# A two-layer hybrid encoder on one core: the norms' 1 / rms through ScalarE's logarithm and exponential instead of Newton steps on VectorE

## The chip, the cores and the metric

The kernel runs on one core of a Trainium2 chip. A core has TensorE (PE, matrix products, with its weight loads listed apart as PEld), VectorE (DVE), ScalarE (ACT), GpSimd (POOL) and SyncE (SP, which here only issues DMAs), each with its own in-order queue of instructions. SBUF holds the working tiles (128 partitions), PSUM the results of TensorE, in banks of 128 x 512 float32. The metric is the device time of one execution in microseconds (us).

## The reference

Two layers of an encoder over 1024 tokens of width 1024, all in float32, and a last norm. Cut to what matters:

```python
def rms_norm(x, g):
    y = x * lax.rsqrt(jnp.mean(x * x, axis=-1, keepdims=True) + EPS)     # EPS = 1e-6
    return y * g

for l in range(DEPTH):                                   # DEPTH = 2
    proj = rms_norm(x, norm1_g[l]) @ w_in[l]
    (a_cq, a_ckv, a_kr, b_q, ..., d_v) = jnp.split(proj, splits, axis=-1)
    y_a = mla_mixer(...)    # latent attention: rms_norm(a_cq) over 192 and rms_norm(a_ckv) over 128 columns first
    y_b = diff_mixer(...)   # w = p0 - lam * p1 per head; rms_norm of each head's 64 outputs, no norm of the group
    y_c = swa_mixer(...)    # window of +-128
    y_d = na_mixer(...)     # 2-D neighbourhood
    mix = concatenate([rms_norm(y_a), y_b, rms_norm(y_c), rms_norm(y_d)])
    x = x + mix @ w_out[l]
    x = x + square(relu(rms_norm(x, norm2_g[l]) @ w_up[l])) @ w_down[l]
return rms_norm(x, final_norm_g)
```

So each layer has norm1, two latent norms, the two pairs of B's heads, the norms of groups A, C and D, and norm2; the final norm closes the kernel.

## The kernel before

Activations lie with features on partitions and the 1024 tokens along the free dimension, eight tiles of 128 x 1024. Every product of float32 operands is made of three passes over a high and a low part of each operand (`passes`, L220 to L222); `split` (L194, L197, L198, and L188, the line of every two-operand operation) makes the parts, the high one on ScalarE, the low one on VectorE or, for weights, on GpSimd.

A layer runs in stages. Projection of group B's six column tiles in two waves (`several`). Attention of B (`attn_b`), and woven into it, as filling, the projections of the latents (`proj_latent`) and of group D. Then attention of D with the projections of C and the latents' up-projections (`latent_up`), attention of C, attention of A, the output projection, and the MLP (`mlp_up`, `mlp_down`), in which sums of blocks replace an eighth of the block products. `weave` takes turns between an attention and its filling; `tick` lets the steps of finished heads (`tails`: `denominators`, `sub_norm`, `mix_group`, `mix_b`) follow one at a time. The written order is not the last word: the kernel is put in order by a planner that simulates the engines with estimated durations before the kernel runs, and so fixes the order of each engine's queue. Only TensorE's order in the MLP is left as written.

A norm over features needs sums across partitions. The squares are summed over the tiles first; `rstd_cols` then multiplies each 128 tokens of them by a column of ones (L261), so that PSUM holds one column per 128 tokens, tokens on partitions: 8 columns for the whole sequence, 16 for two heads at once, 4 for half the sequence. The mean and the small constant are applied on VectorE (L263, or L688 for the latents). `rsqrt_cols` then takes 1 / sqrt of the columns: a first value from the bits of the number (L247, an integer shift in float arithmetic) and three Newton steps of three VectorE operations each (L249, L188, L251). The columns come back to rows in one of two ways. `spread_here` multiplies a broadcast column by the identity (L297) and copies the bank to SBUF (L292): norm1, norm2 and, in `final`, the last norm. `rows_of` transposes the columns (L270), copies (L272) and stores them in DRAM, and `spread` loads the rows broadcast over partitions: the latents, `sub_norm` and `mix_group`.

The latents' sums come from `latent_parts` (L655 and L657) as three small tiles of 8 columns: two of the query latent, to be added, and one of the key-value latent. `proj_latent` ends with both norms (L688 to L689) and stores two sets of rows.

In B's attention, `probs` makes two softmaxes per query tile. `softmax` writes negated scores and their minimum `nm` in one pass on VectorE (L806), after which ScalarE takes the exponential with its sum (L809). The second head's probabilities are scaled by `cb` = z0 * (-lam) / z1, one number per row: a reciprocal (L890) and one more operation (L891) on VectorE, the scaling on ScalarE (L893), the sum on GpSimd. That is 64 times in the kernel.

The functions used on ScalarE are copy, square and exponential; the one table load stands at the kernel's start.

Of the kernel before, what the change touches and what calls it, by code (L numbers as in the profile page):

```python
# [6 lines left out]

# [1 line left out]

# [4 lines left out]
F = mybir.dt.float32  # L14
R = mybir.dt.float32r
I32 = mybir.dt.int32
AF = mybir.ActivationFunctionType
# [6 lines left out]
EPS = 1e-6  # L24
NEG = -1e30
LAYERS = 2


T_CQ, T_CQR, T_CKV = 0, 1, 2
# [116 lines left out]
class Trunk:  # L146
# [91 lines left out]
                                    c == 0 and k == 0, c == 1 and k == 3)  # L238


    def rsqrt_cols(self, ms):

        nc = self.nc
        n = ms.shape[1]
        r = self.cp.tile([P, n], F, tag="rs_r", name="rs_r")
        t = self.cp.tile([P, n], F, tag="rs_t", name="rs_t")
        nc.vector.tensor_scalar(r.bitcast(I32), ms.bitcast(I32), -0.5, 1597463007.0, ALU.mult, ALU.add)  # L247
        for _ in range(3):
            nc.vector.scalar_tensor_tensor(out=t, in0=r, scalar=-0.5, in1=r, op0=ALU.mult, op1=ALU.mult)  # L249
            self.tt(t, t, ms)  # L250
            nc.vector.scalar_tensor_tensor(out=r, in0=t, scalar=1.5, in1=r, op0=ALU.add, op1=ALU.mult)  # L251
        return r

    def rstd_cols(self, sq, count, rhs, tag="mm"):

        nc = self.nc
        g = rhs.shape[1]
        n = sq.shape[1] // P
        ps = self.bank(tag, [P, n * g])
        for t in range(n):  # L260
            nc.tensor.matmul(ps[:, t * g:(t + 1) * g], sq[:, t * P:(t + 1) * P], rhs, start=True, stop=True)  # L261
        ms = self.cp.tile([P, n * g], F, tag="ms", name="ms")
        nc.vector.tensor_scalar(ms, ps, 1.0 / count, EPS, ALU.mult, ALU.add)  # L263
        return self.rsqrt_cols(ms)

    def rows_of(self, col, grid=False):

# [12 lines left out]

    def spread(self, dst, rows, j=0, g=1):

        src = rows.rearrange("(t g) p -> g t p", g=g)[j]
        n = dst.shape[0]
        self.load(dst.rearrange("p (t q) -> p t q", t=8), src.partition_broadcast(n))

    def spread_here(self, dst, col):

# [12 lines left out]
    def setup(self):  # L301
        nc, d = self.nc, self.d
        tile = lambda shape, name, dt=F: self.const.tile(shape, dt, name=name)
        width = d["par"].shape[1]
        par = tile([P, width], "par")
        self.load(par, d["par"])
        self.x, self.first = [], []
        for k in range(8):
            if k < 3:
                self.first.append(self.weights(d["w_in"][0, self.WAVES[0][k], 0]))  # L310
            x = self.xp.tile([P, S], F, tag="x", name=f"x{k}")
            self.load(x, d["x"][k])
            self.x.append(x)
        self.ident = tile([P, P], "ident")
        self.load(self.ident, d["ident"])
        self.ones = tile([P, 2], "ones")
        nc.vector.memset(self.ones, 1.0)
        self.pairs = tile([P, 2], "pairs")
        nc.vector.memset(self.pairs, 0.0)
        nc.vector.memset(self.pairs[0:64, 0:1], 1.0)  # L320
        nc.vector.memset(self.pairs[64:128, 1:2], 1.0)
        self.rb = tile([P, S], "rb")
        self.zero = tile([P, P], "zero", R)
        nc.vector.memset(self.zero.bitcast(F), 0.0)

        at = 0

        def take(*shape):
            nonlocal at
            n = math.prod(shape)  # L330
            v = par[:, at:at + n]
            at += n
            return v.rearrange("p (l k) -> p l k", l=shape[0]) if len(shape) > 1 else v

        L = LAYERS
        self.g1, self.g2, self.gfin = take(L, 8), take(L, 8), take(8)
        self.gout = {n: take(L, 2) for n in ("mla", "swa", "na")}
        self.gkv, self.gq, gsub, self.sink = take(L), take(L, 2), take(L), take(L, 4)
        self.nsink = tile([P, L, 4], "nsink")
        nc.vector.tensor_scalar(self.nsink, self.sink, -1.0, None, ALU.mult)  # L340
        lam = self.rb.rearrange("p (l f) -> p l f", l=L)[:, :, 0:256]
        self.load(lam[:, :, 0:128], d["lam"].rearrange("p (l f) -> p l f", l=L))
        self.gsub = tile([P, L], "g_sub")
        self.nlam = tile([P, L], "nlam")
        e = tile([P, L, 2], "lam_e")
        for l in range(L):
            li = 0.8 - 0.6 * math.exp(-0.3 * l)
            nc.vector.tensor_scalar(self.gsub[:, l:l + 1], gsub[:, l:l + 1], 1.0 - li, None, ALU.mult)
            v = lam[:, l, 128:192]
            self.tt(v, lam[:, l, 0:64], lam[:, l, 64:128])  # L350
            nc.vector.tensor_reduce(out=e[:, l], in_=v.rearrange("p (j f) -> p j f", j=2), axis=AX, op=ALU.add)
            nc.scalar.activation(e[:, l], e[:, l], AF.Exp)
            nc.vector.tensor_scalar(e[:, l, 0:1], e[:, l, 0:1], li, None, ALU.add)
            self.tt(self.nlam[:, l:l + 1], e[:, l, 1:2], e[:, l, 0:1], ALU.subtract)
# [306 lines left out]
    def proj_latent(self, l, one, xs, rb, tabs, lat, krd, rows_out):  # L661


        nc = self.nc
        squares = [self.col("sq%d" % i, 8) for i in range(3)]
        for i, t, g in ((0, T_CQ, self.gq[:, l, 0:1]), (2, T_CKV, self.gkv[:, l:l + 1])):
            yield from one(t, xs, self.ev_plain(rb, lambda n, y: self.latent_parts(y, g, P, n, lat[:, i], squares[i])))
        c, s = tabs

        def ev(n, ps):  # L670
            sl = slice(n * 512, n * 512 + 512)
            y, t2 = self.part(), self.part()
            self.tt(y[0:64], ps[0:64], rb[0:64, sl])
            self.tt(y[64:112], ps[64:112], c[64:112, sl])
            self.tt(t2[64:80], ps[96:112], s[96:112, sl])
            self.tt(t2[96:112], ps[64:80], s[64:80, sl])
            self.tt(y[64:80], y[64:80], t2[64:80], ALU.add, self.eng)
            self.tt(y[96:112], y[96:112], t2[96:112], ALU.subtract, self.eng)
            self.emit_parts(y[64:112], [
                (krd[:, :, h, sl].rearrange("a p s -> p a s"), slice(64 + 32 * h, 80 + 32 * h))  # L680
                for h in range(2)], slice(64, 112))
            self.latent_parts(y, self.gq[:, l, 1:2], 64, n, lat[:, 1], squares[1])

        yield from one(T_CQR, xs, ev)
        q, k = squares[0], squares[2]
        self.tt(q, q, squares[1], ALU.add)
        for m, count in ((q, 192), (k, 128)):
            nc.vector.tensor_scalar(m, m, 1.0 / count, EPS, ALU.mult, ALU.add)  # L688
            rows_out.append(self.rows_of(self.rsqrt_cols(m)))  # L689
        yield True  # L690

    def latent_up(self, l, lat, rows, qa, ka, va):
        nc, d = self.nc, self.d
        rq, rkv = self.big_tile(F, "rq"), self.big_tile(F, "rkv")
        self.spread(rq, rows[0])
        self.spread(rkv, rows[1])
        parts = []
        for i, r in ((0, P), (1, 64), (2, P)):
            p = []
# [165 lines left out]
    def attn_b(self, l, t, qb, kb, vb, out):  # L865
# [3 lines left out]
        def head(h2):  # L869
            if h2 == 0:  # L870
                pair["y"], pair["rz"] = self.ypair(), self.rz_tile()
            y, rz = pair["y"], pair["rz"]
            qk = []
            for c in range(2):
                g = h2 * 2 + c
                q, k = self.stack(), self.stack()
                qf, kf = q.bitcast(F), k.bitcast(F)
                for i, (a, b) in enumerate(((0, 0), (0, 1), (1, 0))):
                    self.load(qf[i * 32:(i + 1) * 32], run(qb[a, t, g]))
                    self.load(kf[i * 32:(i + 1) * 32], run(kb[b, t, g]))  # L880
                qk.append([(q[0:96], k[0:96])])
            v = self.vtile(vb[2 * t + h2])
            z = [self.col("z0", 8), self.col("z1", 8)]

            def probs(qt):
                ps = []
                for c in range(2):
                    ps.append(self.softmax(qk[c], qt, z[c][:, qt:qt + 1], 32 ** -0.5))
                c = self.col("cb")
                nc.vector.reciprocal(c, z[1][:, qt:qt + 1])  # L890
                nc.vector.scalar_tensor_tensor(out=c, in0=z[0][:, qt:qt + 1], scalar=self.nlam[:, l:l + 1], in1=c,  # L891
                                               op0=ALU.mult, op1=ALU.mult)
                nc.scalar.activation(ps[1], ps[1], AF.Copy, scale=c)  # L893
                self.tt(ps[0], ps[0], ps[1], ALU.add, nc.gpsimd)
                return ps[0]

            def done():
                self.tails.append(self.denominators(z[0], rz[h2 * 64:(h2 + 1) * 64]))

            return probs, v, y, h2, done  # L900
# [590 lines left out]
```

## Time and profile before

| | |
|---|---|
| median of 3 runs | 2735.67 us (2726.91 to 2736.3) |
| the profiled execution | 2728.97 us |
| its span, first to last instruction | 2727.2 us |
| mean granted TensorE clock | 0.967 |
| busy: TensorE, VectorE, ScalarE, GpSimd | 2553.1, 1994.1, 1430.9, 1134.5 us |

The rows that follow in the prediction are of four kinds. The first part of the page gives the busy time of each engine with its share of the span and the number of instructions; the fourth gives the shares of the chain of work that ended last. A row of the windows view gives a stretch (start:end, length) and then, for TensorE, its weight loads, VectorE, ScalarE and GpSimd, the busy time with the number of instructions, followed by the granted clock, the share of the DMA engines and GB/s; its last row is the sum. A row of the timeline gives start, duration, engine, line, operation, output<-inputs, shapes and, in brackets, how long the engine stood idle before it and what ended that. A row of the grouped instructions gives count | busy us, mean ns of one | idle time before. The view of one source line gives its durations in ns as least/median/greatest, and who waited for it (us, times).

### The profile page before, as it was taken

The numbers are of one execution on the slowest core, as the hardware profiler recorded it, in microseconds if no ns is written. First come the engines' busy times: TensorE is split into PE (matmuls) and PEld (weight loads), VectorE is DVE, ScalarE is ACT, GpSimd is POOL, SyncE is SP. The second block draws the span as 40 slices with busy tenths as digits, with TensorE's granted clock in tenths as the row PEclk, the third lists the DMA queues.
The fourth block names the chain that finished last, engine by engine and source line by source line (L and its number), as shares of the span: only waits on it lengthen the run. The fifth ranks groups of instructions, "written<-read, shape, count | busy, mean of one in ns | idle before, by whom it ended". The sixth has DMA issues, their size and how long they took to land.

```text
span 2727.2 us, 37613 instructions
## 1 busy us (share of the span) xinstructions
PE 2553.1 (94%) x12298; PEld 2110.1 (77%) x12298; DVE 1994.1 (73%) x3544; ACT 1430.9 (52%) x2547; POOL 1134.5 (42%) x754
## 2 busy tenths in 40 slices
PE   8989988899989999999999899889998999999997
PEld 6778876787778887888877688767886788878886
DVE  7787767674966669787567778677749666687786
ACT  4667757563534444444436676576635344444444
POOL 2555642111245554445435556331013455545552
PEclk9989999999989999999998899899999999999998
DMA  5534597231234447444244345972221444664431
GB/s 175 166 105 126 154 280 241 83 93 40 65 130 156 151 160 267 156 138 142 98 133 138 95 134 157 300 215 71 76 70 44 154 159 149 223 222 150 131 100 62
DMA packets 190516, 389.20 MB, mean 143 GB/s; under 512 B 23712, under 2 KB 30832, under 8 KB 190320
## 3 DMA queue, kind: packets, MB, share of 16 engines
q1 hardware_dynamic: 176496, 361.62, 43.0%
q10 hardware_dynamic: 13824, 25.17, 2.7%
q8 instruction: 98, 1.61, 0.3%
q14 instruction: 98, 0.80, 0.1%
HBM read 263.29 MB, written 123.41 MB: 142 GB/s over the span
## 4 chain that ended last, share of the span: by engine, by line
PE 70%; DVE 14%; DMA 7%; ACT 4%; issue 3%; SPq 1%; POOL 1%; DVEq 0%; ACTq 0%; POOLq 0%
PE u L220 8%; PE u L222 8%; PE u L221 8%; PE mm L220 5%; PE mm L221 5%; PE mm L222 5%; PE p L220 5%; PE p L221 5%; PE p L222 5%; PE sb L804 3%; PE tr L840 2%; DVE p L806 2%; DVE part L188 2%; PE pv L829 2%; PE pv L828 2%
## 5 line engine op out<-in xcount | busy, mean ns | idle before, releaser
L188 POOL TENSOR_TENSOR wl<-raw,wh 128x512 fp32r<-128x512 f32 x448 | 635.1, 1418 | 705.2 <-ACT wh L194 690.1
L194 ACT ACTIVATE wh<-raw 128x512 fp32r<-128x512 f32 x448 | 281.5, 629 | 579.8 <-PE u L221 315.0
L188 POOL TENSOR_TENSOR wl<-ws,wh 128x512 fp32r<-128x512 f32 (+1 forms) x112 | 148.1, 1325 | 456.9 <-ACT wh L194 426.0
L220 PE MATMUL u<-far,wh 128*128 128x512 f32 x768 | 301.5, 393 | 11.5 <-ACT ev L1237 8.3
L188 DVE TENSOR_TENSOR raw<-raw 128x512 f32<-128x512 f32 x256 | 226.4, 890 | 107.4 <-POOL wl L188 56.9
L222 PE MATMUL u<-far,wl 128*128 128x512 f32 x768 | 300.5, 391 | 1.9 <-POOL wl L188 1.9
L221 PE MATMUL u<-far,wh 128*128 128x512 f32 x768 | 300.3, 391 | 0.0
L188 DVE TENSOR_TENSOR ptl<-tr,pth 128x512 fp32r<-128x512 f32 (+2 forms) x384 | 238.3, 628 | 66.6 <-ACT pth L194 64.9
L809 ACT ACTIVATE p<-p,nm 128x1024 f32<-128x1024 f32 x192 | 220.1, 1147 | 99.8 <-DVE nm L806 98.9
L194 ACT ACTIVATE pth<-tr 128x512 fp32r<-128x512 f32 (+2 forms) x384 | 205.6, 546 | 121.0 <-PE tr L840 64.8
L220 PE MATMUL p<-far,wh 128*128 128x512 f32 x640 | 251.7, 393 | 7.6 <-DVE ev L188 7.6
L222 PE MATMUL p<-far,wl 128*128 128x512 f32 x640 | 250.9, 392 | 1.5 <-POOL wl L188 1.5
L221 PE MATMUL p<-far,wh 128*128 128x512 f32 x640 | 251.0, 392 | 0.0
L804 PE MATMUL sb<-stack 96*128 96x512 f32 x640 | 218.5, 424 | 24.7 <-DVE nm L806 24.0
L188 DVE TENSOR_TENSOR far<-act,far 128x512 fp32r<-128x512 f32 x224 | 208.6, 960 | 14.6 <-ACT far L194 14.6
L188 POOL TENSOR_TENSOR p<-p 128x1024 f32<-128x1024 f32 x64 | 154.3, 2415 | 141.1 <-ACT p L893 125.0
L220 PEld LDWEIGHTS u<-far,wh 128*128 128x128 f32 x768 | 145.4, 189 | 43.6 <-ACT ev L1237 9.2
L222 PEld LDWEIGHTS u<-far,wl 128*128 128x128 f32 x768 | 145.0, 189 | 33.2 <-POOL wl L188 2.7
L220 PE MATMUL mm<-xh,wh 128*128 128x512 f32 x416 | 169.4, 407 | 0.8 <-DVE rows L272 0.2
L806 DVE CUSTOM_DVE_ANT_0 p<-sb,zero,nm 128x512 f32<-128x512 f32 x192 | 142.4, 743 | 36.3 <-PE sb L804 32.8
L221 PEld LDWEIGHTS u<-far,wh 128*128 128x128 f32 x768 | 145.3, 189 | 30.2
L221 PE MATMUL mm<-xl,wh 128*128 128x512 f32 x416 | 166.6, 400 | 0.0
(243 smaller groups left out, 6147.0 us busy)
## 6 DMA issues: line engine op xcount, KB each, us to landing
act<-acts SPq DMA_DIRECT2D x224, 256.0 KB
raw<-in_w_up SPq DMA_DIRECT2D x128, 256.0 KB
acts<-ev SPq DMA_DIRECT2D x128, 256.0 KB
raw<-in_w_down SPq DMA_DIRECT2D x128, 256.0 KB
acts<-ev ACTq DMA_DIRECT2D x96, 256.0 KB
ws<-in_w_in SPq DMA_DIRECT2D x76, 256.0 KB
rz<-drows SPq DMA_DIRECT2D x40, 256.0 KB
stack<-kd SPq DMA_DIRECT2D x32, 256.0 KB
```

Source lines behind the costliest of these rows:

```text
L188: (eng or self.nc.vector).tensor_tensor(out=out, in0=a, in1=b, op=op)
L194: nc.scalar.activation(hi, src, AF.Copy)
L220: mm(ps, w[0], x[0][:, sl], start=start, stop=False)
L221: mm(ps, w[0], x[1][:, sl], start=False, stop=False)
L222: mm(ps, w[1], x[0][:, sl], start=False, stop=stop)
L804: self.nc.tensor.matmul(ps, q[:, qt * P:(qt + 1) * P], k[:, sl], start=i == 0, stop=i == len(passes) - 1)
L806: self.nc.vector.tensor_tensor_reduce(out=p[:, sl], in0=ps, in1=self.zero[:, 0:1].bitcast(F).broadcast_to([P, 512]), scale=-scale, scalar= ...
L809: self.nc.scalar.activation(p, p, AF.Exp, bias=nm[:, 1:2], scale=-1.0, accum_out=z)
L828: nc.tensor.matmul(out, v[:, kt], h[:, sl], start=kt == 0, stop=False)
L829: nc.tensor.matmul(out, v[:, kt], lo[:, sl], start=False, stop=kt == 7)
L840: nc.tensor.transpose(t[:, k * 256 + i * P:k * 256 + (i + 1) * P], p[:, (j * 2 + k) * P:(j * 2 + k + 1) * P], self.ident)
```

## The change

`rsqrt_cols` takes the sums and their count. ScalarE makes ln(sum / count + eps), exp(-0.5 of it) and the square of that; VectorE makes the negative half of the mean, and one Newton step of two operations. The sums may lie in PSUM, which both engines then read. One table set with both logarithm and exponential is loaded by an instruction ahead of everything. In `rstd_cols` the columns of two heads are no longer interleaved, so that `spread` reads a head's rows as one piece. The three latent columns become parts of one tile, the key-value sums are scaled by 192 / 128, and one call with one set of rows serves both latents. B's coefficient becomes one operation with two scalar columns, after the reciprocal as before.

```diff
+ACT_SET = [s.name for s in act_sets.SETS].index("natural_log_exp_and_others")
...
-    def rsqrt_cols(self, ms):
+    def rsqrt_cols(self, ss, count):
         nc = self.nc
-        n = ms.shape[1]
-        r = self.cp.tile([P, n], F, tag="rs_r", name="rs_r")
-        t = self.cp.tile([P, n], F, tag="rs_t", name="rs_t")
-        nc.vector.tensor_scalar(r.bitcast(I32), ms.bitcast(I32), -0.5, 1597463007.0, ALU.mult, ALU.add)
-        for _ in range(3):
-            nc.vector.scalar_tensor_tensor(out=t, in0=r, scalar=-0.5, in1=r, op0=ALU.mult, op1=ALU.mult)
-            self.tt(t, t, ms)
-            nc.vector.scalar_tensor_tensor(out=r, in0=t, scalar=1.5, in1=r, op0=ALU.add, op1=ALU.mult)
+        n = ss.shape[1]
+        tile = lambda tag: self.cp.tile([P, n], F, tag=tag, name=tag)
+        ms, r, t = tile("ms"), tile("rs_r"), tile("rs_t")
+        nc.scalar.activation(r, ss, AF.Ln, scale=1.0 / count, bias=self.eps)
+        nc.vector.tensor_scalar(ms, ss, -0.5 / count, -0.5 * EPS, ALU.mult, ALU.add)
+        nc.scalar.activation(r, r, AF.Exp, scale=-0.5)
+        nc.scalar.activation(t, r, AF.Square)
+        self.tt(t, t, ms)
+        nc.vector.scalar_tensor_tensor(out=r, in0=t, scalar=1.5, in1=r, op0=ALU.add, op1=ALU.mult)
         return r
...
-            nc.tensor.matmul(ps[:, t * g:(t + 1) * g], sq[:, t * P:(t + 1) * P], rhs, start=True, stop=True)
-        ms = self.cp.tile([P, n * g], F, tag="ms", name="ms")
-        nc.vector.tensor_scalar(ms, ps, 1.0 / count, EPS, ALU.mult, ALU.add)
-        return self.rsqrt_cols(ms)
+            nc.tensor.matmul(ps.rearrange("p (g t) -> p t g", g=g)[:, t], sq[:, t * P:(t + 1) * P], rhs,
+                             start=True, stop=True)
+        return self.rsqrt_cols(ps, count)
...
-        src = rows.rearrange("(t g) p -> g t p", g=g)[j]
-        n = dst.shape[0]
-        self.load(dst.rearrange("p (t q) -> p t q", t=8), src.partition_broadcast(n))
+        src = rows.rearrange("(g t) p -> g (t p)", g=g)[j]
+        self.load(dst, src.partition_broadcast(dst.shape[0]))
...
-        squares = [self.col("sq%d" % i, 8) for i in range(3)]
+        cols = self.col("sq", 24)
+        both = cols[:, 0:16]
+        squares = [cols[:, i * 8:i * 8 + 8] for i in (0, 2, 1)]
...
         self.tt(q, q, squares[1], ALU.add)
-        for m, count in ((q, 192), (k, 128)):
-            nc.vector.tensor_scalar(m, m, 1.0 / count, EPS, ALU.mult, ALU.add)
-            rows_out.append(self.rows_of(self.rsqrt_cols(m)))
+        nc.vector.tensor_scalar(k, k, 192 / 128, None, ALU.mult)
+        rows_out.append(self.rows_of(self.rsqrt_cols(both, 192)))
...
-        self.spread(rq, rows[0])
-        self.spread(rkv, rows[1])
+        self.spread(rq, rows[0], 0, 2)
+        self.spread(rkv, rows[0], 1, 2)
...
-                nc.vector.scalar_tensor_tensor(out=c, in0=z[0][:, qt:qt + 1], scalar=self.nlam[:, l:l + 1], in1=c,
-                                               op0=ALU.mult, op1=ALU.mult)
+                nc.vector.tensor_scalar(c, c, z[0][:, qt:qt + 1], self.nlam[:, l:l + 1], ALU.mult, ALU.mult)
...
+    nc.scalar.add_instruction(mybir.InstLoadActFuncSet(
+        name=nc.get_next_instruction_name(), act_func_set_id=ACT_SET, engine=mybir.EngineType.Activation))
```

More of the change, by code (lines that the diff above doesn't have):

```diff
@@ L8 @@
 import numpy as np
+import concourse.act_sets as act_sets
 import concourse.bass as bass
@@ L317, in setup @@
         nc.vector.memset(self.ones, 1.0)
+        self.eps = tile([P, 1], "eps")
+        nc.vector.memset(self.eps, EPS)
         self.pairs = tile([P, 2], "pairs")
```

## The prediction

> **What bounds the kernel now.** I read the first part of the page for the engines, then the chain that ended last, then the twenty places where the norms stand, by windows.
>
> ```profile
> PE 2553.1 (94%) x12298; PEld 2110.1 (77%) x12298; DVE 1994.1 (73%) x3544; ACT 1430.9 (52%) x2547; POOL 1134.5 (42%) x754
> PE 70%; DVE 14%; DMA 7%; ACT 4%; issue 3%; SPq 1%; POOL 1%; DVEq 0%; ACTq 0%; POOLq 0%
> ```
>
> TensorE is the bound: 94% busy and 70% of the chain. VectorE work pays only where TensorE stands still for it. So the question is not how many VectorE operations go, but beside which of them TensorE idles. The windows view, cut at the first and last operation of each call of `rsqrt_cols`, answers it. The first row is the sum over twelve calls (norm1 twice, `sub_norm` four times, `mix_group` six times); below it stand the six other places: the latent norms of both layers (the stretch in which VectorE is held), norm2 of both layers, the two halves of the final norm.
>
> ```profile
> sum 54.94, PE 53.65 PEld 45.61 DVE 50.36 ACT 26.66 POOL 11.33; mean PE 4.47 PEld 3.80 DVE 4.20 ACT 2.22 POOL 0.94
> ...
> 163.87:173.64 9.77, 2.16 (x8) 1.14 (x7) 9.77 (x22) 4.27 (x7) 7.77 (x4) 0.67 0.11 27
> 1510.93:1519.31 8.38, 1.95 (x7) 1.14 (x5) 8.31 (x12) 3.25 (x6) 7.46 (x4) 0.50 0.13 47
> 753.46:758.40 4.94, 0.14 (x1) 0.00 (x1) 4.61 (x15) 0.63 (x1) 1.61 (x1) 0.75 0.00 0
> 2099.47:2104.40 4.93, 1.14 (x6) 0.58 (x5) 4.60 (x15) 0.63 (x1) 1.35 (x1) 0.98 0.00 0
> 2691.99:2694.92 2.93, 0.00 (x0) 0.00 (x0) 2.57 (x13) 1.35 (x2) 0.60 (x1) 0.96 0.00 0
> 2713.68:2715.87 2.19, 0.00 (x1) 0.01 (x1) 1.78 (x11) 0.00 (x0) 0.00 (x0) 0.50 0.00 0
> sum 33.14, PE 5.38 PEld 2.88 DVE 31.64 ACT 10.13 POOL 18.79; mean PE 0.90 PEld 0.48 DVE 5.27 ACT 1.69 POOL 3.13
> ```
>
> Twelve calls last 54.94 us and TensorE works through 53.65 of them: covered. The other six last 33.14 us with 5.38 of TensorE: 27.8 us of idle time is all that a norm of no cost could give directly. The granted clock, the column after POOL, is 0.67 and 0.50 in the latent stretches, so what TensorE does there is also slow.
>
> Why the latent norms are so dear shows in the timelines of VectorE and GpSimd in layer 0, then of VectorE in layer 1.
>
> ```profile
> 154.76 1.31 DVE L891 SCALAR_TENSOR_TENSOR cb<-z,nlam,cb 128x1 f32<-128x1 f32 x1
> 162.05 1.29 DVE L891 SCALAR_TENSOR_TENSOR cb<-z,nlam,cb 128x1 f32<-128x1 f32 x1
> 163.87 1.92 DVE L688 TENSOR_SCALAR sq<-sq 128x8 f32<-128x8 f32 x1
> 166.37 1.79 DVE L247 TENSOR_SCALAR rs_r<-sq 128x8 int32<-128x8 int32 x2
> 168.12 2.34 DVE L249 SCALAR_TENSOR_TENSOR rs_t<-rs_r 128x8 f32<-128x8 f32 x2
> 170.42 1.32 DVE L188 TENSOR_TENSOR rs_t<-rs_t,sq 128x8 f32<-128x8 f32 x2
> ...
> 163.40 2.35 POOL L188 TENSOR_TENSOR tabc<-tabc,rb 128x1024 f32<-128x1024 f32 x1
> 165.72 2.33 POOL L188 TENSOR_TENSOR tabs<-tabs,rb 128x1024 f32<-128x1024 f32 x1
> 168.02 2.34 POOL L188 TENSOR_TENSOR p<-p 128x1024 f32<-128x1024 f32 x1
> ...
> 1510.93 1.55 DVE L188 TENSOR_TENSOR sq<-sq,sq 128x8 f32<-128x8 f32 x1
> 1512.52 2.27 DVE L688 TENSOR_SCALAR sq<-sq 128x8 f32<-128x8 f32 x1
> 1514.82 1.32 DVE L247 TENSOR_SCALAR rs_r<-sq 128x8 int32<-128x8 int32 x2
> 1516.26 2.31 DVE L188 TENSOR_TENSOR rs_t<-rs_t,sq 128x8 f32<-128x8 f32 x1
> 1525.08 1.80 DVE L251 SCALAR_TENSOR_TENSOR rs_r<-rs_t,rs_r 128x8 f32<-128x8 f32 x1
> ```
>
> An operation on eight columns takes 1.3 to 2.3 us and ends as the GpSimd operation beside it ends: 163.87 + 1.92 = 165.79 against 163.40 + 2.35 = 165.75. VectorE is held while GpSimd has SBUF, one GpSimd operation for each such VectorE operation. Behind the held ones stand the softmax minima `nm`, for which TensorE waits.
>
> **The change part by part.** Counts first. Before, 20 calls of 11 VectorE operations (mean, shift, nine of Newton) are 220; after, 18 calls of 3 and two scalings of `k` are 56. ScalarE gets 18 x 3 = 54.
>
> ```profile
> L1090 ACT ACTIVATE z<-nb,par 128x8 f32<-128x8 f32 x8 | 2.3, 288 | 0.0
> L352 ACT ACTIVATE lam_e<-lam_e 128x2 f32<-128x2 f32 x2 | 0.4, 192 | 1.3 <-DVE lam_e L351 1.3
> L194 ACT ACT_TABLE_LOAD x1 | 1.3, 1283 | 0.7 <-PEq L1479 0.7
> L809 ACT ACTIVATE p<-p,nm 128x1024 f32<-128x1024 f32 x192 | 220.1, 1147 | 99.8 <-DVE nm L806 98.9 <-DVE cb L890 0.3
> ```
>
> A logarithm with a bias column is priced by the first row (0.288), exponential and square by the second (0.192 each): 0.67 us a call, 12.1 in all, on an engine that is 52% busy: beside other work. Uncontended, the old chain is the last final window, 2.19 us for 11 operations, 0.2 each. The new one is 0.67 + 2 x 0.2 = 1.07 and, with handovers that I estimate at 0.05 each for four of them, 1.3; the mean on VectorE runs beside ScalarE.
>
> *Twelve covered calls: 0.* TensorE's products cover them. Without that cover they would give at most 12 x 0.9 = 10.8; 54.94 - 53.65 = 1.3 is idle there now.
>
> *Latent norms: -9.4.* The joined form leaves, on VectorE, the sum of `q`, the scaling of `k`, the mean, one product and one last step; all touch SBUF with shapes like those that are held above. Idle now is 9.77 - 2.16 = 7.6 and 8.38 - 1.95 = 6.4. Four holds stand in layer 0 (1.92, 1.79, 2.34, 1.32; mean 1.84), five in layer 1 (mean 1.85). I let two holds a layer go (3.7) and two or three stay, as the scaling and the last product meet the same GpSimd queue. Some 17 uncontended operations of 0.2 go too, of which I count 1.0, the rest lying between other VectorE work. That is 4.7 a layer. Ends: 0 if each remaining operation is held as long as GpSimd's queue lasts; 14.0 if all idle time goes. One `rows_of` less a layer takes a small transpose, a copy and one store out of SP's queue: nothing waits for them, 0.
>
> *B's coefficient: -2.2.* The two rows of layer 0 above against the median below.
>
> ```profile
> L891 DVE SCALAR_TENSOR_TENSOR cb<-z,nlam,cb x64: 203/219/2251, 100.6 to 1691.5; 128x1 f32<-128x1 f32 x64
> ...
>   ACT p L893: 20.1, 20
> ...
> 25.25 3.83 POOL L188 TENSOR_TENSOR wl<-ws,wh 128x512 fp32r<-128x512 f32 x2 [4.65 <-ACT wh L194]
> 27.88 0.14 DVE L353 TENSOR_SCALAR lam_e<-lam_e 128x1 f32<-128x1 f32 x1
> ```
>
> The old form reads two SBUF columns and is held up to 2251 ns. The new one is a TENSOR_SCALAR on one column; the only such row beside a GpSimd operation (27.88, inside 25.25 to 29.08) took 0.14 us, not held. So 1.31 + 1.29 - 2 x 0.219 = 2.2 us go where TensorE has least cover. ScalarE waited for `cb` 20 times, 20.1 us; elsewhere TensorE hides that. Ends: 0 and 5. The Trainium skill, GPSIMD Engine Reference, section Specifications, says that GpSimd shares its SBUF interfaces with VectorE, with contention for VectorE instructions that have two SBUF inputs or run in a 2-port mode. The holds above agree. VectorE: DVE Perf Modes, section What auto-detection actually checks, would let a one-source operation with equal source and destination in SBUF take such a mode; by that the new coefficient is held like the old and this term is 0. The row at 27.88 speaks against it, once.
>
> *Norm2: -4.2.* TensorE waits for the last Newton step.
>
> ```profile
> 754.57 1.23 DVE L188 TENSOR_TENSOR rs_t<-rs_t,ms 128x8 f32<-128x8 f32 x1
> ...
> 758.40 3.78 PE L297 MATMUL mm<-ident,rs_r 128*128 128x128 f32 x16 [4.80 <-DVE rs_r L251]
> 2104.40 3.58 PE L297 MATMUL mm<-ident,rs_r 128*128 128x128 f32 x16 [3.79 <-DVE rs_r L251]
> ...
> 2694.92 2.08 PE L297 MATMUL u<-ident,rs_r 128*128 128x128 f32 x8 [3.52 <-DVE rs_r L251]
> 2715.87 2.08 PE L297 MATMUL u<-ident,rs_r 128*128 128x128 f32 x8 [2.22 <-DVE rs_r L251]
> ```
>
> Eight operations of 0.2 go in each (1.6), and layer 0's one hold (1.0). ScalarE is free there: 0.63 of 4.94 us. The four other VectorE operations in the window stay, before or after. Ends: 0 and 8.6 (both waits).
>
> *Final: -1.9.* Second half 2.19 to 1.3, -0.9. First half 2.93, where ScalarE is busy 1.35 and one other VectorE operation stands between: I take -1.0. Ends 0 and 3.1, in which 2.5 is both at 1.3.
>
> *`spread` in one piece:* in `sub_norm` 64 rows x 8 pieces x 2 x 4 calls, 4096 pieces of 512 bytes, become 512 of 4 KB; same bytes, and TensorE waits for none by the rows above: 0.
>
> *Table:* the load at the start replaces the one of 1.283 us: 0.
>
> *Waits added:* the logarithm waits on ScalarE with softmax exponentials behind it; the product `t` x `ms` waits on VectorE for the square, with `nm` behind it; the sums' PSUM bank is held until both engines have read it. Priced as a rival.
>
> Sum: 9.4 + 2.2 + 4.2 + 1.9 = 17.7. The profiled execution took 2728.97 (span 2727.2): it would become 2711.3. The median of the runs shown is 6.7 higher, 2735.67; on it, 2718. The ends together are 0 and 30.7. A difference of 0.5%, 13.7 us, is about what a measurement of this kernel tells from none.
>
> **The rivals.**
>
> *The hold moves, it does not go.* GpSimd's two tables and `p` take 7 us in one piece; if VectorE meets them with the scaling, the mean and the products, each is held as now, and `cb` too. For it: one hold per GpSimd operation, whatever the VectorE operation. Against: five touches in place of 23. Left are 4.2 + 1.9: 2729.6, no change.
>
> *ScalarE's queue holds VectorE.* In the attention stages the three steps stand between exponentials of 1.147 us. If logarithm and square each wait for one more, 14 calls (twelve covered, two latent) cost 2.3 each, 32.1 us of VectorE in order with `nm` behind: 2735.67 - 17.7 + 32.1 = 2750, slower. It eats the gain from 1.26 us a call and makes the kernel slower by 0.5% from 2.2. Against: ScalarE is 52% busy, TensorE covers twelve of these calls, and the planner sees ScalarE's durations.
>
> *The table is reloaded.* If logarithm and exponential don't stay in one set, 18 x 2 loads of 1.283 are 46 us of ScalarE; on the six exposed places 6 x 2.57 = 15.4 eats most of the gain: 2733, no change. The Trainium skill, ScalarE: Activation LUTs, sections What ACT_TABLE_LOAD costs and Table sets, gives 2.66 us for a switch with its drain, which would make that 6 x 5.3 = 32 and the kernel 2750; it also lists a set with both functions, which speaks for one load. The trace has a single load and cannot tell.
>
> **How the numbers follow.** My forecast (own range 2702 to 2722): 0.54. The hold that moves: 0.27. Reload: 0.05. ScalarE's queue: 0.14. Faster is the first, no change the second and third, slower the last. The planner orders all engines anew from other durations, which no row prices; it widens the range, 2702 to 2741, which holds the first three cases and leaves the upper part of the last out.
>
> **What would show it.** Right: one table load; `L249` gone; TensorE's waits for `rs_r` at norm2 under 3 us, at the end under 2; the wait of `sb` for `nm` near the latent norm halved, with the granted clock up; `cb` without rows over 0.4 us. Wrong: new waits of VectorE for ScalarE's square, waits for a bank at the sums, operations on 16 columns held over 1 us, or idle TensorE time in stages that the change doesn't touch.

## The result, and the profile after

| | before | after |
|---|---|---|
| median of five runs each | 2729.88 us (2725.18 to 2736.3) | 2709.37 us (2705.89 to 2711.95) |
| the profiled execution (span) | 2728.97 (2727.2) | 2709.95 (2707.9) |

The ratio is 0.9916, 95% interval [0.9899, 0.9934]: 20.5 us faster by the medians, against a forecast of 17.7. By the ratio it is 22.9 us, with an interval from 18 to 27.6. The sum came out nearly as predicted; the runs below show that its parts did not.

The text below speaks of four stages of a layer. Stage B runs from the start of ScalarE's first scaling by the coefficient to the end of its last; D from there to the end of D's last exponential; C and A from there to the ends of C's and A's last exponentials.

First the page of after: busy times, then the grouped instructions of the new form.

```profile
PE 2549.6 (94%) x12296; PEld 2112.5 (78%) x12296; DVE 1943.0 (72%) x3379; ACT 1439.8 (53%) x2601; POOL 1130.9 (42%) x754
...
L1492 ACT ACT_TABLE_LOAD x1 | 1.3, 1283 | 0.7 <-PEq L1484 0.7
L250 ACT ACTIVATE rs_r<-mm,eps 128x8 f32<-128x8 f32 x10 | 2.6, 262 | 8.6 <-PE mm L265 8.6
L252 ACT ACTIVATE rs_r<-rs_r 128x8 f32<-128x8 f32 x10 | 2.1, 206 | 0.3
L253 ACT ACTIVATE rs_t<-rs_r 128x8 f32<-128x8 f32 x10 | 2.1, 210 | 0.3
...
L190 DVE TENSOR_TENSOR rs_t<-rs_t,ms 128x16 f32<-128x16 f32 x6 | 4.4, 736 | 0.4 <-ACT rs_t L253 0.3
L255 DVE SCALAR_TENSOR_TENSOR rs_r<-rs_t,rs_r 128x16 f32<-128x16 f32 x6 | 3.4, 564 | 0.1
L251 DVE TENSOR_SCALAR ms<-sq 128x16 f32<-128x16 f32 x2 | 2.8, 1398 | 0.0
L190 DVE TENSOR_TENSOR rs_t<-rs_t,ms 128x8 f32<-128x8 f32 x10 | 2.7, 273 | 1.9 <-ACT rs_t L253 1.9
```

VectorE is 51.1 us less busy (1994.1 before) and ScalarE 8.9 us more. There is one table load. ScalarE's three steps take 262, 206 and 210 ns. In the two rows of `rs_t<-rs_t,ms`, the idle time behind the last bar is what VectorE waited for the square: 0.3 and 1.9 us. Operations on 16 columns are held still, with means of 0.56 to 1.40 us where the latents' product of layer 1, with no GpSimd operation beside it, takes 0.16 us. Three of the latents' lasted over 1 us (2.30, 1.77 and 2.27 us), which the prediction had listed as a sign of being wrong.

B's coefficient, in the view of its line (ns least/median/greatest; then who waited for it), and in a second fence TensorE's waits (us in total, times, longest):

```profile
L897 DVE TENSOR_SCALAR cb<-cb,z,nlam x64: 252/272/275, 99.5 to 1673.2; 128x1 f32<-128x1 f32 x64
...
  ACT p L898: 11.1, 13
```

```profile
PE sb L810 <- DVE nm L812: 21.4, 22, 4.6
PE mm L299 <- DVE rs_r L255: 5.7, 2, 3.2
PE mm L265 <- DVE sq L190: 4.1, 2, 3.8
PE u L299 <- DVE rs_r L255: 3.9, 2, 2.6
```

None of the 64 is held (20 of them took over 0.4 us before, the longest 2251 ns). The waits for `rs_r` are 5.7 us at norm2 and 3.9 us at the end. Before they were:

```profile
PE sb L804 <- DVE nm L806: 24.0, 20, 5.7
PE mm L297 <- DVE rs_r L251: 8.6, 2, 4.8
PE u L297 <- DVE rs_r L251: 5.7, 2, 3.5
```

At norm2 VectorE's stretch from the mean to the last step lasted 4.94 and 4.93 us before (two of the six places in the prediction). In after:

```profile
743.83:747.10 3.27, 0.81 (x4) 0.35 (x2) 3.27 (x7) 0.63 (x1) 1.86 (x1) 1.00 0.00 0
2083.70:2086.88 3.18, 0.01 (x1) 0.00 (x0) 3.18 (x7) 0.50 (x1) 1.30 (x1) 0.84 0.00 0
```

Next the stretches at the latent norms, a part of layer 0 and one of layer 1, by windows: two rows of before, then two of after.

```profile
170.00:190.00 20.00, 16.32 (x76) 13.39 (x77) 16.68 (x55) 10.79 (x16) 6.45 (x4) 0.77 0.20 48
1500.00:1530.00 30.00, 19.62 (x80) 13.83 (x79) 27.86 (x69) 17.24 (x28) 20.01 (x12) 0.67 0.37 106
```

```profile
170.00:190.00 20.00, 20.00 (x96) 16.76 (x95) 12.96 (x35) 12.54 (x21) 7.35 (x5) 0.89 0.24 66
1500.00:1530.00 30.00, 26.12 (x122) 21.19 (x121) 22.70 (x57) 20.75 (x35) 19.75 (x10) 0.85 0.32 93
```

TensorE gains 3.7 and 6.5 us of busy time in these 50 us, and the granted clock goes from 0.77 and 0.67 to 0.89 and 0.85. The longest wait for `nm` is 4.6 us still, where half of 5.7 had been expected.

Last the stages that the prediction had no term for: attention of C, then of A, in layer 0 and layer 1, cut at the exponentials' ends. First before (layer 1, then layer 0), then after (layer 0, then layer 1).

```profile
1771.20:1840.80 69.60, 58.51 (x305) 46.52 (x306) 53.89 (x146) 49.05 (x126) 20.73 (x12) 0.93 0.74 216
1840.80:1973.40 132.60, 126.33 (x779) 108.24 (x778) 101.39 (x236) 85.69 (x153) 12.81 (x8) 1.00 0.26 75
415.40:479.30 63.90, 54.19 (x294) 42.20 (x293) 49.53 (x142) 45.53 (x122) 12.36 (x8) 0.95 0.73 229
479.30:627.80 148.50, 135.69 (x806) 114.50 (x805) 109.86 (x246) 90.09 (x160) 21.53 (x12) 0.97 0.26 78
```

```profile
411.10:486.40 75.30, 62.88 (x318) 50.02 (x317) 52.97 (x140) 49.51 (x129) 20.67 (x12) 0.89 0.72 217
486.40:618.30 131.90, 125.84 (x773) 107.50 (x772) 100.06 (x228) 86.64 (x156) 12.33 (x8) 1.00 0.25 73
1753.00:1824.30 71.30, 57.58 (x305) 45.43 (x305) 51.77 (x138) 49.54 (x128) 20.71 (x12) 0.95 0.72 210
1824.30:1956.80 132.50, 126.44 (x779) 108.32 (x778) 100.05 (x228) 86.81 (x157) 12.33 (x8) 1.00 0.26 76
```

Before, layer 0 took 63.9 + 148.5 = 212.4 us for what layer 1 did in 202.2. In the long form GpSimd works 21.5 us in stage A instead of 12.8, four operations more: two of group D's norm (`y`), one of C's (`yc`) and one part of a weight, which in the short form come in C. After has the short form in both layers (207.2 and 203.8).

### The profile page after: what moved, and what is told of

The parts are those of the page before. It is cut to its first block, busy times and chain, and to the rows that moved or that the text cites. A ratio compares the mean times of both kernels' runs of the same rounds, so it can differ in the third digit from the quotient of the medians.

```text
span 2707.9 us, 37502 instructions
## 1 busy us (share of the span) xinstructions
PE 2549.6 (94%) x12296; PEld 2112.5 (78%) x12296; DVE 1943.0 (72%) x3379; ACT 1439.8 (53%) x2601; POOL 1130.9 (42%) x754
## 4 chain that ended last, share of the span: by engine, by line
PE 73%; DVE 12%; DMA 6%; ACT 4%; issue 3%; POOL 1%; SPq 0%; DVEq 0%; ACTq 0%; POOLq 0%
PE u L222 8%; PE u L224 8%; PE u L223 8%; PE mm L222 5%; PE mm L223 5%; PE mm L224 5%; PE p L222 5%; PE p L223 5%; PE p L224 5%; PE sb L810 3%; PE tr L846 3%; DVE p L812 2%; DVE part L190 2%; PE pv L835 2%; PE pv L834 2%
```

## The experiments

Each kernel ran in alternation with before, whose median was 2729.61, 2730.39 and 2730.86 us in the three sessions. Differences in us are worked out from the ratios; the medians differ from that by up to 4 us. The theory is the prediction's: shorter chains where TensorE stands still. The rival is that the planner's new order decides, whatever the arithmetic. The kernels with the new form in some of the norms have after's layout of two heads' columns too, which is then tried by itself.

### Parts alone

**B's coefficient alone** (`e1_cb_alone`): before with

```diff
-nc.vector.scalar_tensor_tensor(out=c, in0=z[0][:, qt:qt + 1], scalar=self.nlam[:, l:l + 1], in1=c, ...)
+nc.vector.tensor_scalar(c, c, z[0][:, qt:qt + 1], self.nlam[:, l:l + 1], ALU.mult, ALU.mult)
```

> The kernel before with B's coefficient alone in the new form. Theory (holds and exposed waits): no coefficient is held any more (longest of the 64 under 0.3 us, before 2.25), some 11 us of VectorE time go, but TensorE covers most of it: 2 us faster, between 0 and 5. Rival (the planner's new order decides, not the operations): the time differs from before by anything up to 10 us, either sign, and in stages after group B's attention.

Measured: 2743.73 us, ratio 1.0056 [1.0038, 1.0074], slower, although its 64 coefficients are free of holds too. The theory's 2 us faster missed; the rival's order fits, with more than its 10 us. Both layers have the long form of C and A (214.4 and 216.5 us). Stage B takes 238.1 and 242.6 us, against 237.4 and 244.9: 1.6 us less together.

**All norms, with the old coefficient** (`e2_norms_alone`): after with that line put back.

> The changed kernel with B's coefficient back in its old form, so the norms alone. Theory: 18 us faster than before (the 20.5 of the whole change less 2 for the coefficient), with coefficients held up to 2 us again. If the coefficient matters more than that, under 14. Rival (order): no relation, between 5 and 25.

Measured: 2723.88 us, ratio 0.9984 [0.9972, 0.9996], 4 us faster where 18 had been expected. Taken from the whole change, the coefficient is worth 19 us (14.5 by the medians); added to before, it costs 15. No sum of parts gives both. Stage B is 479.0 us in the two layers, 5.8 more than after's.

**The latent norms alone** (`e3_latents_alone`): the joined call in `proj_latent`, the old Newton steps in `rstd_cols`, the old coefficient.

> The kernel before with the joined latent norms by logarithm and exponential alone; all other norms keep their three Newton steps. Theory: 8 to 9 us faster, gained in group B's attention of both layers (before it -0, after it -3 in layer 0 and -8 in layer 1), nothing later. Rival (the holds by GpSimd only move to other operations): 0 to 3 faster.

Measured: 2712.77 us, ratio 0.9943 [0.9924, 0.9962], 16 us and more than half of the whole, where 8 to 9 had been expected. The places are not those expected either: stage B became 3.7 us longer in layer 0 and 11.8 shorter in layer 1, and C and A, where nothing was expected, are short in both layers (203.2 and 205.8).

**All but the latents** (`e4_all_but_latents`): after with the two old latent norms.

> The changed kernel with the latent norms back to two calls of three Newton steps. Theory: 12 us faster than before: norm2 3 to 4, final 2 to 3, the coefficient 2, norm1 1, and 4 to 5 between the ends of group D's and group A's attention in layer 0, where the whole change gained 5 us that the sum did not have. If that last gain hangs on the latents' place in the order, 8 faster and no gain there.

Measured: 2721.93 us, ratio 0.9966 [0.9954, 0.9979], 9 us faster; C and A take 214.5 and 211.7 us. So the gain in C and A of layer 0 hangs on the latents' place in the order, as the second case of the expectation has it. Stage B, in which the latents are the old ones here, took 474.2 us, as little as with the latents alone (474.2) and 1.0 more than in after.

**Norm2 and the final norm alone** (`e5_norm2_final_alone`): in `rstd_cols`, `return self.rsqrt_cols(ps, count)` for these two, the Newton steps for the rest.

> The kernel before with the new 1 / rms at norm2 and at the final norm only; latents, covered norms and B's coefficient as before. The weave is that of before (31 and 57 products left). The prediction's terms for these are -4.2 and -1.9 us, 6.1 together: 2724 us (2719 to 2728). Rival 'the wait is VectorE's order there and not the length of the chain': norm2 gives under 1 us a layer and the total is 2727 to 2731.

Measured: 2722.18 us, ratio 0.9973 [0.9957, 0.9989], 7.4 us. This agrees with the 6.1 predicted, and in the profile the changed places hold it: stage A's end to norm2 gave 1.7 and 2.4 us, the final norm 3.4. The profiled span fell by more, 11.6 us, of which 6.2 stand in stage B of layer 1, whose code is unchanged.

**The twelve covered calls alone** (`e6_covered_ticks65`), with the tick rate explained next.

> The kernel before with the new 1 / rms in the twelve calls that the prediction took as covered (norm 1, B's sub norm, the mix norms), with their layout, and D's mix stepped 0.65 times a step of attention C, which leaves 34 and 60 products (before 31 and 57), so that stages C and A are at about before's lengths (212 and 202 us). The prediction's term is 0: 2729 us (2724 to 2734). Rival 'the covered calls are worth something': norm 1's 1.5 us in each layer and the mixes that TensorE waits for at the start of A: 2720 to 2726.

Measured: 2722.88 us, ratio 0.9981 [0.9967, 0.9995], 5.2 us. Again 6.2 us stand in stage B of layer 1: before is the longest of all 14 profiles there. Norm1 itself gave 0.8 us in layer 0, less than the 1.3 us by which that place differs among kernels with the old norm1. The total is the rival's, its places are not: C and A took 210.8 and 202.9.

**The layout alone** (`e9_layout_alone`): before with

```diff
-        src = rows.rearrange("(t g) p -> g t p", g=g)[j]
...
+        src = rows.rearrange("(g t) p -> g (t p)", g=g)[j]
...
```

the load's destination to match, and the sums' columns written head by head.

> The kernel before with only the layout: two heads' columns lie head by head, so that the broadcast of a norm's rows is read in 4 KB pieces and not in 512-byte pieces. No arithmetic changes. Theory 'order of the weave': 31 and 57 products left as in before, so stages C and A as before, and 2729 us (2724 to 2734). Rival 'the smaller number of packets brings the mixes earlier': each broadcast lands 0.5 to 1.5 us sooner, and with the waits of the weave 3 to 8 us are gained: 2722 to 2727.

Measured: 2729.88 us, ratio 1.0004 [0.999, 1.0018]. The time and the stages stay as the theory has them, the rival's 3 to 8 us did not come, and the prediction's 0 for `spread` stands. It is also nearly a repeat of before, and a measure of what one profile can tell: stage B of layer 1 is 2.6 us shorter in it, C and A 3.3 and 2.1 longer.

### What sets stages C and A

After group D's attention its mix norm is carried on by `tick`, a step at a time, while attention of C runs; `EV` says how many ticks come to one step of an attention (0.7 in C). As soon as D's mix is there, the first output groups, products that need it, are woven in. TensorE's queue is in order, and the planner fixes it ahead: I counted how many of attention C's 80 banded products (`pv`) in a layer stand behind the first product of the output groups. (The expectations say 160, which is C's two layers together.) Before has 31 left in layer 0 and 57 in layer 1, after 51 and 57, the coefficient alone 31 and 31. Two kernels change that count with one number and no arithmetic.

**The coefficient alone, ticks 0.75** (`f1_cb_ticks75`):

```diff
-    EV = (.5, .5, .7, 1)
+    EV = (.5, .5, .75, 1)
```

> The kernel before with the new coefficient of B alone, which took 2743.7 us, and one number more changed: group D's mix norm is stepped 0.75 times a step of attention C instead of 0.7. Theory 'order of the weave': what sets stages C and A is how many of attention C's 160 banded products still stand behind the first product of the output groups that need D's mix in TensorE's order. With 31 to 34 left C and A took 212 to 216.5 us together, with 40 left 208 to 212, with 50 or more 202 to 207. This kernel has 40 left in layer 0 and 51 in layer 1 where the coefficient alone had 31 and 31, so it expects C and A at 208 to 212 and 202 to 207 us (214.4 and 216.5 with the coefficient alone), and 2728 us (2722 to 2734). Rival 'the new coefficient itself costs', by its operations on VectorE in stage B: the loss stays, 2744 us (2740 to 2748).

Measured: 2720.76 us, ratio 0.997 [0.9955, 0.9985]: 23 us less than with 0.7, and the loss is gone. C and A take 212.2 and 198.2 us. The rival, that the coefficient itself costs, is refuted. The total lies below the range expected, as do C and A of layer 1; what the coefficient is worth at these ticks stays open, as no kernel has them with the old one.

**Before, ticks 0.65** (`f2_before_ticks65`):

> The kernel before, with the arithmetic of all norms and of B's coefficient untouched; only group D's mix norm is stepped 0.65 times a step of attention C instead of 0.7. It leaves 34 and 34 of attention C's products behind the first output group where before left 31 and 57. Theory 'order of the weave': layer 1's C and A go from 202.2 us to 212 to 216, layer 0's stay at 212 to 215, so 2741 us (2737 to 2748). Rival 'the arithmetic decides, not the order': within 4 us of before, 2726 to 2734.

Measured: 2727.62 us, ratio 0.9997 [0.9984, 1.001]. The stage that was to change did, C and A of layer 1, from 202.2 to 213.6 us; layer 0 has 210.6. The total did not follow: it lies where the rival had it. Stages B and D of layer 1 became 5.1 and 4.0 us shorter in the same profile. So the theory holds for the stages that it names, and even a change of one tick rate shifts others. Even the holds moved: of VectorE's operations for the two latent norms in layer 1, 5 took over 0.4 us in before (9.2 us together) and 2 here (2.5 us), with the same code.

Windows of C and A of layer 1, first of the coefficient alone, then with the ticks at 0.75:

```profile
1775.30:1843.80 68.50, 56.04 (x301) 44.30 (x300) 49.88 (x142) 46.15 (x122) 12.33 (x8) 0.92 0.66 208
1843.80:1992.00 148.20, 135.64 (x802) 114.45 (x801) 109.53 (x245) 89.78 (x159) 21.51 (x12) 0.97 0.26 76
```

```profile
1767.00:1834.40 67.40, 58.03 (x310) 45.15 (x310) 52.88 (x146) 49.23 (x127) 21.35 (x12) 0.95 0.77 233
1834.40:1965.20 130.80, 125.33 (x772) 107.38 (x772) 101.43 (x236) 85.59 (x152) 12.77 (x8) 1.00 0.26 74
```

And the longest of TensorE's waits in the two A windows, in the same order:

```profile
PE mm L220 <- ACT mixh L197: 3.4, 1, 3.4
PE mm L221 <- DVE mixl L198: 2.2, 2, 1.5
PE mm L270 <- DVE rows L272: 1.5, 1, 1.5
```

```profile
PE tr L840 <- DVE ptl L188: 1.2, 3, 0.6
PE pv L828 <- DVE yc L188: 0.8, 1, 0.8
```

With the groups late in the queue, TensorE waits for D's rows and for both parts of its mix (`mixh`, `mixl`), 7.1 us at the head of A. With the groups earlier, these waits are gone. Over 14 profiles and two layers, C and A together took:

| products left | stages | mean, us | from, to |
|---|---|---|---|
| 31 to 34 | 10 | 213.4 | 210.6, 216.5 |
| 40 to 43 | 5 | 209.6 | 206.4, 212.2 |
| 50 to 60 | 13 | 204.2 | 198.2, 208.3 |

In before, C and A of layer 0 lasted 10.2 us longer than in layer 1: by the windows above TensorE idled 5.2 us more and was busy 5.0 us more, at a granted clock that fell for a time (last section). The ranges of neighbouring rows overlap, so the count is a guide, not a price. The rate moves D's mix and the groups together, so which of the two TensorE feels is not separated.

### What holds VectorE, and what is left

**Latents through PSUM** (`f3_latents_psum75`): after, ticks 0.75, and the latents' scaled mean and exponential in a PSUM bank, with a logarithm and a mean for each latent in place of the scaling of `k`.

```diff
+        ps = self.bank("mm", [P, 2 * n])
+        ms, r = ps[:, 0:n], ps[:, n:2 * n]
...
+            nc.vector.tensor_scalar(ms[:, sl], ss, -0.5 / count, -0.5 * EPS, ALU.mult, ALU.add)
+        nc.scalar.activation(r, t, AF.Exp, scale=-0.5)
```

> The kernel after, with two edits: the latent norms write their scaled mean and the exponential to a PSUM bank, so that none of the VectorE operations between the exponential's logarithm and the rows has both its source and its result in SBUF; and D's mix steps at 0.75 (40 and 50 products left behind the first output group, after 51 and 57). Theory 'VectorE's SBUF-to-SBUF operations wait for the GpSimd operation that runs': the multiply and the last step of each latent norm, held up to 2.30 and 1.77 us in after, take under 0.5 us here; the latents' rows come 2 to 4 us earlier in each layer; stage B 1 to 4 us shorter, C and A of layer 0 0 to 5 us longer by the order: 2709 us (2700 to 2716). Rival 'they wait for something else that comes late (their own queue)': the same operations still show rows over 1 us, and nothing is gained: 2710 to 2718.

The timeline of VectorE in after at layer 0's latent norm, with GpSimd below:

```profile
160.68 0.52 DVE L251 TENSOR_SCALAR ms<-sq 128x16 f32<-128x16 f32 x1
164.09 2.30 DVE L190 TENSOR_TENSOR rs_t<-rs_t,ms 128x16 f32<-128x16 f32 x1
166.93 1.77 DVE L255 SCALAR_TENSOR_TENSOR rs_r<-rs_t,rs_r 128x16 f32<-128x16 f32 x1
...
161.25 2.37 POOL L190 TENSOR_TENSOR tabc<-tabc,rb 128x1024 f32<-128x1024 f32 x1
163.58 2.78 POOL L190 TENSOR_TENSOR tabs<-tabs,rb 128x1024 f32<-128x1024 f32 x1
166.33 2.34 POOL L190 TENSOR_TENSOR p<-p 128x1024 f32<-128x1024 f32 x1
```

and in the kernel with PSUM:

```profile
162.66 0.17 DVE L267 TENSOR_SCALAR mm<-sq 128x8 f32<-128x8 f32 x1
163.57 0.16 DVE L267 TENSOR_SCALAR mm<-sq 128x8 f32<-128x8 f32 x1
169.38 0.16 DVE L190 TENSOR_TENSOR rs_t<-rs_t,mm 128x16 f32<-128x16 f32 x1
170.18 0.16 DVE L271 SCALAR_TENSOR_TENSOR rs_r<-rs_t,mm 128x16 f32<-128x16 f32 x1
...
163.23 2.37 POOL L190 TENSOR_TENSOR tabc<-tabc,rb 128x1024 f32<-128x1024 f32 x1
165.55 2.81 POOL L190 TENSOR_TENSOR tabs<-tabs,rb 128x1024 f32<-128x1024 f32 x1
168.32 2.37 POOL L190 TENSOR_TENSOR p<-p 128x1024 f32<-128x1024 f32 x1
```

GpSimd works on in both. The same product takes 2.30 us with two SBUF inputs and 0.16 with one of them in PSUM: the hold is shown. In layer 1 the sum of `q`, left in SBUF, was still held (1.75 us). Stage B took 233.2 and 236.4 us (235.5 and 237.7 after). The total is as expected, and did not move: 2709.48 us, ratio 0.9932 [0.9915, 0.9949]. The free operations stand behind other VectorE work instead: the mean is ready at 163.7, the product comes at 169.38. And C and A of layer 0 took 209.7 us with 40 products left.

**Norm2 ahead in the order** (`g1_norm2_first`): after with

```diff
+            with tc.high_priority(offset=200):
-            r = self.rstd_cols(acc, DM, self.ones[:, 0:1])
+                r = self.rstd_cols(acc, DM, self.ones[:, 0:1])
```

> The kernel after with one edit: norm2's rsqrt is put ahead in the planner's order, so that VectorE does not work on rows of the MLP between the norm's own operations. The weave of attention C is that of after (51 and 57 products left). Theory 'what is left of norm2's wait is VectorE's order': in after TensorE waits 3.2 and 2.5 us there for the norm's last operation, while VectorE spends 4.7 us on five rows of the MLP in between; here both waits are under 1 us, 4 us less in all: 2705 us (2701 to 2708). Rival 'the next thing is as late' (the copy of the broadcast, the late rows of the MLP): the waits move behind the norm and the time is that of after, 2709 (2706 to 2712).

The edit changed nothing: the order of every engine's queue is that of after, and TensorE waits 5.3 us at norm2 (5.7). So the question stays open, and the run is a repeat of after: 2704.17 us, ratio 0.9917 [0.9895, 0.994], with a profiled execution whose span is 6.1 us longer than after's. Stage D alone differs by 3.7 and 3.4 us between these two executions of one program, stage B by 0.4 and 0.1.

**All together** (`g2_all`): after with PSUM latents, that same edit, and ticks at 2.

> All that the runs pointed to, on the kernel after: latent norms through a PSUM bank, norm2's rsqrt ahead in the order, D's mix stepped twice a step of attention C (43 and 54 products left). If the parts add: after's 2709 less 2 us a layer in stage B, less 4 us at norm2, with 0 to 4 us more in layer 0's C and A: 2703 us (2697 to 2710). Rival 'they do not add', since each new order moves the stages by up to 10 us: 2708 to 2720.

Measured: 2710.62 us, ratio 0.9936 [0.9916, 0.9956]. Stage B is the shortest of all, 231.5 and 234.5 us, 7.2 less than after's together; D is 10.5 us longer (79.8 and 82.9, of which the repeat above had 7.1) and C and A 3.7. The rival holds: the parts don't add. As the edit at norm2 does nothing, 4 us of the expected sum could not come. No version beat after beyond its interval.

## Why the prediction was right, step by step

The profiles of before and after have a near twin each (the layout alone; the repeat), so each place has two differences in us:

| place | predicted | before to after | twin to twin |
|---|---|---|---|
| stage B (latents 9.4, coefficient 2.2) | -11.6 | -9.1 | -6.3 |
| stage A's end to norm2's first copy of the broadcast | -4.2 | -3.2 | -3.3 |
| final norm (first sums' end to the end of the span) | -1.9 | -3.4 | -1.6 |
| stages C and A | 0 | -3.6 | -9.1 |
| stage D | 0 | -1.1 | +6.0 |
| all else, with norm1 | 0 | +1.1 | -0.3 |
| span | -17.7 | -19.3 | -14.6 |

The 14 kernels also fall into groups by what they have in stage B. The sum over both layers, in us:

| stage B | old coefficient | new coefficient |
|---|---|---|
| two norms by Newton steps | 476.5 to 482.3 (5 kernels) | 474.2 to 481.0 (3) |
| joined norm | 474.2 and 479.0 | 473.2 and 473.7 |
| joined norm through PSUM | none | 466.0 and 469.6 |

- **Latent norms, -9.4: the mechanism came, its worth was mis-sized.** The prediction let two holds a layer go, 7.4 us of VectorE's time. Operations of the two norms that took over 0.4 us fell from 9 (16.3 us) to 5 (8.7 us), and those that were let stay did stay. But it counted VectorE's time in full as TensorE's: TensorE's waits for `nm` in the 50 and 65 us around the norms fell from 6.8 and 6.4 us to 4.9 and 4.8, 3.5 us in all. In stage B the joined norm is worth 8.1 us added to before and 1.0 us added to the rest of the change. The reason given for the holds, GpSimd's operation beside them, is shown by the PSUM form, in which the same steps pass beside such an operation in 0.16 us.
- **Coefficient, -2.2: the mechanism came, its worth is not separated.** No row is over 275 ns, and ScalarE's waits for the coefficient's last operation fell from 20.1 to 11.1 us. In stage B the new form is worth 1.6 us added to before and 5.8 us added to the norms alone. With neither edit stage B is 478.9 us in the mean, with both 473.5: 5.4 us less, for the two terms of 11.6 together. Between kernels with neither edit it differs by 5.8.
- **Norm2, -4.2, and final, -1.9: right, and the best shown.** Seven kernels have Newton steps at these places and seven the new form. Stage A's end to norm2 took 265.3 to 266.9 us in both layers together with the old, 261.2 to 263.5 with the new, 3.6 less in the mean; the final norm 33.9 to 35.8 and 32.3 to 34.2, 2.2 less. The waits fell by 2.9 and 1.8 us (8.6 to 5.7, 5.7 to 3.9), a little short of "under 3 us each" and "under 2": the longest are 3.2 and 2.6 us. The eight operations gave the 1.6 us a layer (4.9 to 3.3 and 3.2). The 1.0 us for layer 0's hold did not come: one operation there is held for 1.25 us, before 1.23. VectorE also still works on rows of the MLP between the norm's steps.
- **Twelve covered calls, 0, and idle time in untouched stages.** Where they stand they are covered. What was missing is a term for where the planner puts the next thing: group D's mix fell into the short form in layer 0. The prediction named a new order as unpriced and listed "idle TensorE time in stages that the change doesn't touch" as a sign against it; such stages did change, to its favour by 4 to 9 us.
- **`spread`, 0, and table, 0: right.** The layout alone is 1.0004; one load.
- **Rivals.** "ScalarE's queue holds VectorE" asked for 32.1 us; VectorE's waits for the square are 1.9, 0.3 and 0.5 us in all. The mean, which the prediction let run beside ScalarE's steps, starts in 17 of 18 calls only after the logarithm has ended; VectorE idled 27.7 us ahead of the means, against 24.9 us in the kernel before, where it waited for TensorE's sums. "The hold moves" is half true: the joined norm has fewer holds, and those that are left are as long. "Slower" did occur, for the coefficient alone, by the weave and not by the mechanism given.

So the total agreed partly by luck: stage B gave 2.5 to 5.3 us less than its terms, stages C and A 3.6 to 9.1 that no term held. Twins, even of one program, differ by as much as the smaller terms; only where many kernels share a place, as at norm2, is a term of some 4 us tested by itself.

## What to carry to other kernels

Where a planner orders the queues, test the parts alone and together, and before crediting an edit with a gain look at stages that it doesn't touch: find what waits in the in-order queue (here output groups for a mix) and count what stands behind it. A hold read from one profile belongs to one order: a tick rate alone changed 9.2 us of held latent operations to 2.5. A waiting operation on a side engine is worth something only where the bounding engine's wait ends with it, so price it by that wait and not by its own length. To free a small VectorE operation from GpSimd, keep one operand or the result in PSUM; here that shortened stage B by 3.6 us in one kernel and 7.2 in the other, and the total by nothing that could be measured.

## What the hardware showed unexpectedly

- One operand or the result in PSUM frees a VectorE operation from GpSimd: thirteen such rows of the latents that ran beside a GpSimd operation in the two PSUM kernels took 0.16 to 0.17 us, where SBUF forms of 8 and 16 columns took up to 2.38 (norm2 and final norm alone).
- A TENSOR_SCALAR from SBUF to SBUF is held with 16 columns (0.52 and 2.27 us, `ms`) but not with one: 64 coefficients within 252 to 275 ns, 21 of them overlapping a GpSimd operation. The Trainium skill, VectorE: DVE Perf Modes, section What auto-detection actually checks, has one-source operations in SBUF take a 2-port mode when the outermost dimensions of more than one element are both even or equal. The 16-column rows agree with that. A one-column operation has no such dimension, so the prediction's reading, by which the new coefficient would be held, goes further than the section.
- More idle time in stage A came with a lower granted clock: in the 13 of 28 stages A with 5.2 to 6.4 us of idle TensorE time it was 1.000 throughout, in the 15 with 7.0 to 12.8 us 0.954 to 0.987. In the long stage A of before (12.8 us of idle in 148.5) it stood at 0.50 for 10.2 us, around the waits for `mixh` (3.8 us) and `mixl` (2.3 us) at its head. Which of the two brings the other is not tested:

```profile
489.70:499.90 10.20, 6.56 (x15) 4.34 (x16) 7.92 (x7) 4.09 (x6) 5.67 (x3) 0.50 0.17 51
```
